# A hybrid mLSTM and attention block on one core: gates computed in the v/o projections, down weights requested earlier, stores of ScalarE's results issued on ScalarE's queue

## The chip, the cores and the metric

The kernel runs on one core of a Trainium2 chip. The metric is the device time of one execution in microseconds; the kernel before takes 3026.59 us, the median of three runs (3026.36 to 3028.20). Another execution, taken with the hardware profiler, gives the trace that all rows below come from.

## The reference

One layer of a bidirectional encoder for 2048 tokens of width 1024, all in float32:

```python
h = x
xn = rms_norm(h, ln_mix_g)
proj = xn @ w_in                                  # 2512 columns: q, k, v, o, gates, c_q, c_kv, k_rope
y_a = mlstm_group(q, k, v, o, gates + b_gates)    # 4 heads of 128, both directions, chunks of 128
y_b = mla_group(c_q, c_kv, k_rope, w_uq, w_ukv)   # 4 heads, softmax over all 2048 keys
h = h + concatenate([y_a, y_b]) @ w_out
h = h + (silu(conv3(xn2 @ w_up_gate)) * conv3(xn2 @ w_up_val)) @ w_down     # 2816 columns
h = h + sigmoid(rms_norm(h, ple_norm_g) @ w_ple_gate) * rms_norm(p @ w_ple_proj, ple_post_g)
return rms_norm(h, final_g)
```

The mLSTM's q and k go through a convolution over three tokens and a SiLU before use. Its gates (4 heads, two directions, an input and a forget gate) go through a logarithm of a sigmoid, running sums and running maxima along the tokens.

## The kernel before

Every large product is made of three matmuls (`mm3`, L127 to L132): both operands are split into a rounded high part and a rest, and high times high, high times low and low times high are added up in one PSUM bank. The split of an operand (`split`, L112, or `split_g`, which also scales) is a cast on ScalarE (L116 or L124) and a subtraction on VectorE (L119 or L125). Row L129 of a profile is therefore a matmul of any stage, and L116 and L119 are the splits of any operand; the tile names tell them apart: `wsp` and `xh`/`xl` are weights and x in the first projection, `woa`, `wq`, `cq` the operands of the side jobs, `q_t` the queries, `pt` transposed probabilities, `fw` the weights of the feed-forward part, `hid` its hidden values.

Intermediate results go to tensors in HBM (names that end in `_d`) and are read back when a later stage wants them. All transfers, loads and stores, are issued by SyncE (SP), which runs its instructions in program order: a transfer whose data or buffer is not ready holds up all that stand behind it. [...]

A scheduler sets the order of each engine's instructions from its own estimate of times, except for TensorE within `manual_schedule` (from L400 on, the q/k projection), where TensorE keeps the order of the code. Buffers are named places (`x0` to `x15`, `w0` to `w13`, `t0` to `t7`, `s0` to `s2`, `u0` to `u2`); a place is taken over by a new tile when the readers of the old one are done.

The stages, with their place in the profiled execution:

- `in_proj`, first part (0 to 120 us): x arrives transposed (`load_x`, L219), is squared (`x_sq`) for the row norms, split, and multiplied with the last 464 columns of w_in. `rest(st)` makes one row tile of 128 tokens; `turn_rest` (L275) transposes its results and stores them to `rest_d`.
- v and o projections (L315 to L331, 120 to 291 us): 16 row tiles each; `nat` makes the 24 matmuls of one tile.
- q/k projection (L333 to L436, 291 to some 520 us): for each of eight column groups j and four token ranges c, `block(j, c)` makes 24 matmuls, and `conv(j, c)` the three taps, the SiLU and the store to `qk_d` (L396). Between matmuls, `pump` (L368) draws steps from a chain of generators, `side`: `absorb` (L488: products of up-projection weights, stored to `wo_d`, L529), `gates` (L602: the scalar chain of the mLSTM gates, with matmuls on TensorE at L624, L640, L666, L676, L681, L701 and L707 that transpose or spread small tiles) and `q_up` (L533: queries for attention, stored to `q_d`). A `yield` ends a step; `pause(n)` is n empty steps. Each call of pump adds 1.26 steps, and there are four calls in a block. What is left of `side` after block(6, 2) is run off at once (L412).
- attention (`attend`, L926, some 520 to 1270 us): 64 query tiles (4 heads of 16) in turn. For each tile: four score banks on TensorE (`score_bank`), their maxima on VectorE (L884), exponentials on ScalarE (L902), transposes (L942), the split of `pt`, and after two tiles the products with the values (`pv`), whose result ScalarE copies to `ya` (L958) and SP stores with two DMAs to `y_d` (L960). Query tiles are loaded by `load_q` (L863) into `q_t`. Between them a slower pump draws steps from `tail` (L438) and `mlstm` (L711): a backward pass over 15 chunks, which stores transposed keys to `kn_d` (L761), and a forward pass over 16 chunks, which stores its result `hy` to `y_d` (L850).
- `out_proj` (1270 to 1450 us): the output projection, and the norm and transposition of its rows (`transpose_out`, L1038 to L1051), stored to `x2_d`.
- `up` (L1271, 1450 to 2290 us): 44 pairs of a gate and a value column group, each of seven products (`prod`) named after their operands. A pair's last products and its convolution (`rest`, `conv`) run within the next pair. `conv` works in two buffers `fgv` (w7 for the gate, w11 for the value), multiplies them into the value's one and stores it to `hid_d` (L1318). After the last pair, `down_weights` (L1409) starts the loads and splits of the first two down weights (`wd0`, L1393).
- `down` (2290 to 3027 us): 22 down weights times hidden values (`facc`) for each of four token ranges; in the last one the per-layer embedding is begun.

## Time and profile before

| what | us |
|---|---|
| median of three runs | 3026.59 |
| the profiled execution | 3029.05 |
| its span, first to last instruction | 3027.3 |
| TensorE busy (matmuls) | 2975.4 |
| VectorE busy | 1890.7 |
| ScalarE busy | 1360.7 |
| mean granted clock of TensorE, of full speed | 0.995 |

A wait in the profile is idle time of an engine just before an instruction, put down to what released that instruction. In a list of waits a row names the engine, the result and line of the instruction that waited, and the instruction it waited for, with the us in total, the number of times and the longest of them. In a table of windows a row gives a stretch in us from the span's start, its length, the busy time and number of instructions of five engines (TensorE's matmuls, its weight loads, VectorE, ScalarE, GpSimd), the clock granted to TensorE, the busy share of the DMA engines and the rate in GB/s.

### The profile page before, as it was taken

What the parts mean: (1) busy time and instruction counts of PE and PEld (TensorE: products, weight loads), DVE (VectorE), ACT (ScalarE), POOL (GpSimd) and SP (SyncE); (2) the same over time, 40 slices, a digit from 0 to 9 for tenths busy, and PEclk for the clock granted to TensorE, in tenths of its full rate; (3) what the DMA queues carried; (4) which work ended last, traced back from release to release, by engine and by line L of the source; (5) the groups of instructions that cost most, each with busy time, mean ns of one, the idle gap of its engine ahead of it and who ended that gap; (6) DMA issues with size and microseconds to landing.
All of it is one profiled execution on the core that took longest, in us unless ns stands there. A gap on an engine that the chain in (4) does not pass through costs nothing. (4 is left out here: it accounts for less than half of the span.)

```text
span 3027.3 us, 40574 instructions
## 1 busy us (share of the span) xinstructions
PE 2975.4 (98%) x15122; PEld 2510.5 (83%) x15122; DVE 1890.7 (62%) x3441; ACT 1360.7 (45%) x2602; POOL 142.0 (5%) x262
## 2 busy tenths in 40 slices
PE   8999999999999999999999999999999999999998
PEld 7888788898988888888778877888887888888887
DVE  7321655777776777646888888777776343334565
ACT  7211544555665566423534446444444332223443
POOL 3100000000000000001000000000000000000111
PEclk9999999999999999999999999999999999999999
DMA  6522345343323243568753335433337565444221
GB/s 194 110 70 96 109 135 162 121 150 107 105 93 93 96 126 114 178 207 274 229 194 134 135 135 194 140 122 123 124 122 233 164 221 199 146 155 148 79 79 63
DMA packets 322901, 430.03 MB, mean 142 GB/s; under 512 B 24960, under 2 KB 218512, under 8 KB 322704
## 3 DMA queue, kind: packets, MB, share of 16 engines
q1 hardware_dynamic: 322704, 427.44, 44.0%
q8 instruction: 119, 1.95, 0.3%
q14 instruction: 78, 0.64, 0.1%
HBM read 292.17 MB, written 135.20 MB: 141 GB/s over the span
## 5 line engine op out<-in xcount | busy, mean ns | idle before, releaser
L129 PE MATMUL facc<-fw,hid 128*128 128x512 f32 x2112 | 480.8, 389 | 3.7 <-ACT fw L116 2.6
L129 PEld LDWEIGHTS facc<-fw,hid 128*128 128x128 f32 x2112 | 396.0, 188 | 87.3 <-ACT fw L116 3.0
L129 PE MATMUL fxy<-oph,fw 128*128 128x512 f32 x1408 | 451.9, 394 | 6.0 <-DVE ug L1363 5.1
L129 PEld LDWEIGHTS fxy<-oph,fw 128*128 128x128 f32 x1408 | 265.7, 189 | 76.0 <-DVE ug L1363 11.7
L119 DVE TENSOR_TENSOR fw<-fwr,fw 128x1024 fp32r<-128x1024 f32 x176 | 215.1, 1222 | 166.8 <-ACT fw L116 166.6
L116 ACT CAST fw<-fwr 128x1024 fp32r<-128x1024 f32 x176 | 184.9, 1051 | 260.1 <-PE facc L129 131.4
L129 PE MATMUL fxy<-opl,fw 128*128 128x512 f32 x704 | 276.1, 392 | 0.0
L129 PE MATMUL bk<-wsp,xh 128*128 128x512 f32 (+1 forms) x768 | 235.9, 388 | 1.0 <-DVE wsp L125 1.0
L129 PE MATMUL fzs<-oph,fw 128*128 128x512 f32 x704 | 234.3, 389 | 0.9 <-DVE xt L1117 0.9
L116 ACT CAST pt<-tb 128x512 fp32r<-128x512 f32 x256 | 146.6, 586 | 195.2 <-PE tb L942 194.5
L884 DVE TENSOR_REDUCE mx<-bk 128x1 f32<-128x512 f32 x256 | 174.5, 684 | 48.3 <-PE bk L883 47.2
L129 PE MATMUL ppv<-pt,kv 128*128 128x256 f32 x1536 | 204.5, 287 | 0.0
L119 DVE TENSOR_TENSOR pt<-tb,pt 128x512 fp32r<-128x512 f32 x256 | 173.7, 684 | 36.9 <-ACT pt L116 35.0
L129 PEld LDWEIGHTS ppv<-pt,kv 128*128 128x128 f32 x1536 | 189.1, 191 | 0.3 <-ACT pt L116 0.3
L902 ACT ACTIVATE pe<-bk,nm 128x512 f32<-128x512 f32 x256 | 174.1, 695 | 24.5 <-DVE nm L896 23.7
L129 PE MATMUL pgp<-pw,x3s 128*128 128x512 f32 (+1 forms) x792 | 178.7, 385 | 0.0
L129 PE MATMUL bk<-wo,yhl 128*128 128x512 f32 x744 | 175.5, 392 | 0.0
L129 PEld LDWEIGHTS bk<-wsp,xh 128*128 128x128 f32 x768 | 145.4, 190 | 27.8 <-DVE wsp L125 2.7
L129 PEld LDWEIGHTS pgp<-pw,x3s 128*128 128x128 f32 x792 | 144.4, 188 | 28.3
L129 PEld LDWEIGHTS bk<-wo,yhl 128*128 128x128 f32 x744 | 138.2, 188 | 28.0
L129 PE MATMUL bk<-xh,wqk 128*128 128x512 f32 x480 | 159.0, 397 | 0.0
L129 PE MATMUL bk<-wsp,xl 128*128 128x512 f32 (+1 forms) x384 | 150.4, 392 | 8.0 <-ACT wsp L124 7.6
(324 smaller groups left out, 5363.5 us busy)
## 6 DMA issues: line engine op xcount, KB each, us to landing
fwr<-in_w_down SPq DMA_DIRECT2D x88, 512.0 KB, 3.6
fwr<-in_w_up SPq DMA_DIRECT2D x66, 512.0 KB, 4.1
s_d<-fwr SPq DMA_DIRECT2D x44, 512.0 KB, 3.3
fws<-s_d SPq DMA_DIRECT2D x44, 512.0 KB, 3.6
hraw<-hid_d SPq DMA_DIRECT2D x33, 512.0 KB, 4.3
rw<-row_d SPq DMA_DIRECT2D x32, 512.0 KB, 5.2
hid_d<-fgv SPq DMA_DIRECT2D x22, 512.0 KB, 3.5
hid_d<-fgv SPq DMA_DIRECT2D x22, 511.5 KB, 5.1
```

The source lines that it names most:

```text
L116: nc.scalar.copy(hi, src)
L119: (sub or nc.vector).tensor_tensor(lo, src, _f(hi), op=ALU.subtract)
L129: mm = lambda *a, **k: self.nc.tensor.matmul(*a, **k, skip_group_check=more)
L884: nc.vector.tensor_reduce(s.mx[:, kb:kb + 1], ps, axis=AX.X, op=ALU.max)
L902: nc.scalar.activation(s.pe[:, kb % 2], s.banks[kb], AF.Exp, bias=s.nm, scale=ASCALE, accum_out=s.rs[:, kb:kb + 1])
```

## The change

- `load_x(0)` is made with two DMAs of half the tile.
- `gates` is no longer part of `side`: a step of it is drawn after each row tile of the v projection from the third on and after each of the o projection; what is left is run off after these. Its own pauses are cut, its scratch tiles move from w5, w7, w8 and t6 to u0, u1, u2 and t4. `pump` adds 0.96 steps in place of 1.26; `absorb` begins with five empty steps in place of three, and its second result buffer moves from t7 to w2.
- `conv` is cut into `taps` (up to the SiLU) and `silu` (with the store). For the last column group, the three that were left at the end of the projection become steps of `tail`, hence side jobs of attention.
- 166 stores are issued by ScalarE (`nc.scalar.dma_start`): `rest_d`, `qk_d`, `wo_d`, `kn_d`, `y_d` of the mLSTM, `y_d` of attention, and `x2_d` in `out_proj`.
- In `up`, the two `fgv` buffers change places from pair to pair, and the product is written over the gate's.
- The first two down weights are requested within the last pair, the first after the product S1·T1 and the second after S2·T2, in places x13 and x14 (before x14 and x15), and no longer after the loop.

```diff
         def load_x(st):
-            nc.sync.dma_start(t, d["x_turned"][:, :, st * P:(st + 1) * P])
+            for f in range(1 if st else 2):
+                fs = slice(0, KT) if st else slice(4 * f, 4 * f + 4)
+                nc.sync.dma_start(t[:, fs], d["x_turned"][:, fs, st * P:(st + 1) * P])
...
-            nc.sync.dma_start(self.rest_d[:, :, st * P:(st + 1) * P], rt)
+            nc.scalar.dma_start(self.rest_d[:, :, st * P:(st + 1) * P], rt)
...
+        gates = self.gates()
...
             nc.sync.dma_start(self.v_d[st], t)
+            if st >= LAG_R:
+                next(gates, None)
...
             nc.sync.dma_start(self.o_d[st], t)
+            next(gates, None)
+        for _ in gates:
+            pass
...
-        side = chain(self.absorb(), self.gates(), self.q_up())
+        side = chain(self.absorb(), self.q_up())
...
-            due[0] += 1.26
+            due[0] += 0.96
...
+            silu(j, c, taps(j, c))
+
+        def taps(j, c):
             t = self.at(next(trot), [P, 512], name="ct")
...
+            return t
+
+        def silu(j, c, t):
             nc.scalar.activation(t, t, AF.Silu)
-            nc.sync.dma_start(self.qk_d[4 * c:4 * c + 4, :, j, :].rearrange("c p t -> p c t"),
+            nc.scalar.dma_start(self.qk_d[4 * c:4 * c + 4, :, j, :].rearrange("c p t -> p c t"),
...
             block(7, 1, self.gbank)
-            conv(7, 2)
             next(att)
             block(7, 0, self.gbank)
-            conv(7, 1)
-            conv(7, 0)
 
         def tail():
             for i in range(2):
                 self.split_kv(vals, (2 + i,))
                 yield
+            ts = []
+            for c in (2, 1, 0):
+                ts.append(taps(7, c))
+                yield
+            for c, t in zip((2, 1, 0), ts):
+                silu(7, c, t)
             yield from pause(6)
...
     def absorb(self):
-        yield from pause(3)
+        yield from pause(5)
...
-                o = self.at(f"t{6 + hf}", [P, 512], name="woo")
+                o = self.at(("t6", "w2")[hf], [P, 512], name="woo")
                 nc.scalar.copy(o, ps)
-                nc.sync.dma_start(self.wo_d[h, :, fs], o)
+                nc.scalar.dma_start(self.wo_d[h, :, fs], o)
...
     def gates(self):
-        mem = [self.at(f"w{i}", [P, 8, P], name="gtmp") for i in (5, 7, 8)]
-        mem.append(self.at("t6", [P, 4, P], name="gtm6"))
+        mem = [self.at(f"u{i}", [P, 8, P], name="gtmp") for i in range(3)]
+        mem.append(self.at("t4", [P, 4, P], name="gtm4"))
...
-        yield from pause(8)
+        yield
         pt = self.pml.tile([P, 2, 16], F32, name="gps", tag="ml")
         nc.tensor.matmul(pt, sel, mg, start=True, stop=True)
...
-            nc.sync.dma_start(self.kn_d[c], kk[:, 0])
+            nc.scalar.dma_start(self.kn_d[c], kk[:, 0])
...
-            nc.sync.dma_start(self.y_d[c, :, 0:4, :], hy[:, 1])
+            nc.scalar.dma_start(self.y_d[c, :, 0:4, :], hy[:, 1])
...
-                    nc.sync.dma_start(self.y_d[2 * pr + i, :, 4 + h, :], rb[:, i])
+                    nc.scalar.dma_start(self.y_d[2 * pr + i, :, 4 + h, :], rb[:, i])
...
     def transpose_out(self, xn, otag, dst, two=True):
-        nc.sync.dma_start(dst, xo)
+        nc.scalar.dma_start(dst, xo)
...
-                t = self.at(("w7", "w11")[half], [P, 2 * SB], name="fgv")
+                t = self.at(("w7", "w11")[half ^ s.i % 2], [P, 2 * SB], name="fgv")
...
-            tt(ts[1], ts[1], ts[0], op=ALU.mult)
+            tt(ts[0], ts[1], ts[0], op=ALU.mult)
...
             prod(s.z, s.ops["S1"], "T1")
+            if i == n - 1:
+                self.wdown = self.down_weights()
+                self.wd0 = [self.wdown(0)]
...
             prod(s.y, s.ops["S2"], "T2")
+            if i == n - 1:
+                self.wd0.append(self.wdown(1))
...
-        self.wdown = self.down_weights()
-        self.wd0 = [self.wdown(c) for c in range(2)]
         rest(prev)
         conv(prev)
...
     def down_weights(self):
-        self.wdrot, self.rrot = _rot("x", (14, 15, 13, 10, 11)), _rot("w", (0, 1))
+        self.wdrot, self.rrot = _rot("x", (13, 14, 15, 10, 11)), _rot("w", (0, 1))
```

The other pauses of `gates`, of two, three and six steps, become one step each or go; the rest of the diff puts the new product's name into the stores of `hid_d`.

More of the change, by code (lines that the diff above doesn't have):

```diff
@@ L621, in to_units @@
             V.tensor_copy(g.rearrange("p (r c h) -> p r h c", r=2, h=4), gt[:, :, f])
-            yield from pause(2)
+            yield
             pt = pbank()
@@ L663, in gates @@
         V.tensor_scalar(mg[:, 1], cm, g[:, P - 1:P], None, op0=ALU.mult)
-        yield from pause(8)
+        yield
         pt = self.pml.tile([P, 2, 16], F32, name="gps", tag="ml")
@@ L673, in gates @@
         flip(o, b)
-        yield from pause(3)
+        yield
         pt = self.pml.tile([P, 16], F32, name="gps", tag="ml")
@@ L694, in gates @@
             nc.sync.dma_start(self.row_d[:, i], o)
-        yield from pause(6)
+        yield
         for n, t in (("w", wl), ("e", em)):
@@ L698, in gates @@
             flip(o, t)
-            yield from pause(2)
+            yield
             pt = pbank()
@@ L704, in gates @@
         V.tensor_copy(sb, so.broadcast_to([P, P]))
-        yield from pause(2)
+        yield
         pt = pbank()
@@ L1315, in conv @@
                 ts.append(t)
-            tt(ts[1], ts[1], ts[0], op=ALU.mult)
+            tt(ts[0], ts[1], ts[0], op=ALU.mult)
             if b:
-                nc.sync.dma_start(self.hid_d[c, :, 2 * SB - 1:4 * SB - 1], ts[1])
+                nc.sync.dma_start(self.hid_d[c, :, 2 * SB - 1:4 * SB - 1], ts[0])
             else:
-                nc.sync.dma_start(self.hid_d[c, :, 0:2 * SB - 1], ts[1][:, 1:])
+                nc.sync.dma_start(self.hid_d[c, :, 0:2 * SB - 1], ts[0][:, 1:])
         def turn(s, f):
```

## The prediction

> **What bounds the kernel now.** I read the page's busy times first, then the waits of TensorE's matmuls by engine and line, then busy time by windows around the longest of these waits, and last the rows of single lines.

> ```profile
> span 3027.3 us, 40574 instructions
> PE 2975.4 (98%) x15122; PEld 2510.5 (83%) x15122; DVE 1890.7 (62%) x3441; ACT 1360.7 (45%) x2602; POOL 142.0 (5%) x262
> ```

> TensorE is busy for 98% of the span. The change removes no matmul, so all it can gain is in the 52 us in which TensorE has none (3027.3 − 2975.4), and in what a low clock adds to the busy time. The waits, as us in total, times, longest:

> ```profile
> PE bk L129 <- ACT wsp L124: 7.6, 1, 7.6
> PE fxy L129 <- DVE ug L1363: 5.1, 5, 3.1
> PE tb L942 <- DVE pt L119: 3.5, 11, 0.5
> PE bk L879 <- ACT pe L902: 3.4, 3, 2.5
> PE gps L666 <- DVE mg L662: 2.9, 1, 2.9
> PE facc L129 <- ACT fw L116: 2.6, 1, 2.6
> ...
> PE mb L738 <- issue: 2.1, 1, 2.1
> PE ssp L234 <- DVE x_ss L231: 1.9, 3, 1.5
> PE gb L512 <- DMA uqt<-in_w_uq_turned: 1.6, 1, 1.6
> PE gb L129 <- DVE woa L119: 1.4, 3, 0.8
> ...
> PE gps L701 <- DVE cols L702: 0.8, 1, 0.8
> ...
> PE gps L640 <- DVE u L372: 0.8, 1, 0.8
> ```

> These are few single events, not a steady loss. Five of them cost more than their length. The windows behind them (us; busy time and count of PE, PEld, DVE, ACT, POOL; the granted clock; DMA share and rate) show it, with two of the gaps themselves:

> ```profile
> 336.90:340.30 3.40, 3.40 (x9) 2.79 (x10) 0.50 (x3) 0.76 (x1) 0.00 (x0) 0.50 0.31 82
> 535.80:538.00 2.20, 0.08 (x2) 0.09 (x1) 2.09 (x7) 1.68 (x3) 0.00 (x0) 1.00 1.05 325
> 538.30:545.10 6.80, 6.21 (x18) 4.78 (x18) 2.64 (x7) 3.22 (x10) 0.00 (x0) 0.50 0.00 0
> 921.00:923.70 2.70, 0.19 (x2) 0.10 (x1) 0.80 (x3) 1.24 (x5) 0.00 (x0) 1.00 0.32 129
> 924.00:927.40 3.40, 3.40 (x10) 2.63 (x9) 0.76 (x2) 2.98 (x14) 0.25 (x2) 0.50 0.13 39
> 1575.90:1579.30 3.40, 3.40 (x9) 2.62 (x10) 3.40 (x5) 0.00 (x0) 0.00 (x0) 0.50 0.21 63
> 2292.70:2296.10 3.40, 3.40 (x9) 2.61 (x8) 3.40 (x4) 0.57 (x1) 0.00 (x0) 0.50 0.63 195
> ```

> After a gap of 2.5 to 3.1 us the clock is at 0.50 for 3.40 us (after the one at 535.8 for 6.80), in which TensorE does half its work: each such window costs another 1.7 us, the long one 3.4. So a gap that goes takes its window along. [...]

> **1. The gates move out of the q/k projection.** Before, this scalar chain ran between q/k matmuls, as a side job at 1.26 steps for each call of pump; after, it runs in the v/o projections, one step for each row tile, and pump goes at 0.96. The chain had waits of 2.9 (L666), 0.8 (L640) and 0.8 (L701), and behind the first lies the window at 336.9 (1.7): 6.2 us. Its new place, and the old one behind it:

> ```profile
> 206.00:291.00 85.00, 85.00 (x376) 70.09 (x375) 16.47 (x32) 16.18 (x32) 0.00 (x0) 1.00 0.25 87
> 323.00:358.00 35.00, 30.23 (x128) 23.90 (x127) 26.61 (x82) 17.46 (x29) 0.00 (x0) 0.95 0.30 86
> ```

> VectorE has work for 19% of the o projection, but for 76% of the stretch where the gates were. One row tile of the projection takes 85/16 = 5.3 us of matmuls, and VectorE's own part of it is 16.47/16 = 1.0. The longest link of the chain runs from the last gate's transposition to the matmul of L666, in the new order two row tiles, 10.6 us:

> ```profile
> L652 DVE SCALAR_TENSOR_TENSOR gtmp<-gtmp 128x128 f32<-128x128 f32 x8 | 2.3, 292 | 0.3
> ...
> L647 DVE RECIPROCAL gtmp<-gtmp 128x128 f32<-128x128 f32 x1 | 1.0, 952 | 0.0
> ```

> With these, some 14 more steps like those of L652 (14 × 0.29 = 4.1) and two tiles' own work (2.0) it comes to 9.4, and an exponential on ScalarE stands in it: there is hardly 1 us to spare, but a link that misses its tile delays TensorE only by the excess. I take no new wait (bounds 0 and the old 2.9 + 1.7). The absorbed weights start three pauses later, so the load of uqt is there when L512 wants it: 1.6. The woa waits (1.4) come from splits that are due every few steps; at 0.96 in place of 1.26 steps they have 31% more time: I take 1.2 of them. Against that, the side jobs now need 102 steps and get 104 × 0.96 = 99.8, so the last three are run off at once behind the last block that feeds them, and the transposes of qsr wait there for a VectorE chain with nothing between: bounds 0 and 2.9 (the longest that a VectorE chain held TensorE up here, L666), I take 1.2. **Sum of 1: −6.2 − 1.6 − 1.2 + 1.2 = −7.8**, between −9.0 and −1.5 (new waits of 2.9 + 1.7 in the o projection and 2.9 behind the drain, instead of 1.2).

> **2. Down weights asked for earlier.** In before, the first two down weights are split behind hid, and TensorE waits for the cast of the first:

> ```profile
> 2289.11 1.05 ACT L116 CAST hid<-hraw 128x1024 fp32r<-128x1024 f32 x1 [2.77 <-DMA hraw<-hid_d]
> ...
> 2291.29 1.99 ACT L116 CAST fw<-fwr 128x1024 fp32r<-128x1024 f32 x2
> ```

> ScalarE idles 2.77 us, casts hid, then does the first step of the last pair's convolution, and only then casts the two weights. Their loads depend on nothing made here. In the new order they are requested within the last pair, after two of its seven products, in buffers x13 and x14 that these products have released, and cast before hid, so TensorE needs no more than the one cast of hid at 2289.11 and can begin when that is done, some 2 us sooner, with more matmuls of this kind to do first: the 2.6 and its window (1.7) go. I take −3.8, leaving 0.5 for VectorE's part of hid; bounds −4.3 and 0 (if hid alone, whose load landed only for 2289.11, ends the same wait).

> **3. Stores on ScalarE's queue.** First the gain: SP issues all loads and stores in order, and a store at the head holds the loads behind it until ScalarE has made its data. The gap at 921 is such a case:

> ```profile
> 916.32 0.32 SPq L863 DMA_DIRECT2D q_t<-q_d  x1
> ...
> 922.46 0.40 ACT L116 CAST q_t<-q_t 128x256 fp32r<-128x256 f32 x1 [3.12 <-DMA q_t<-q_d]
> ```

> ScalarE sat 3.12 us before a cast whose load SP issued only at 916.32; the exponentials behind it, which give TensorE a score bank back, had to wait for it in ScalarE's order. What held SP:

> ```profile
> SPq L863 <- PE bk L883: 91.9, 25, 14.3
> ...
> SPq L960 <- ACT ya L958: 63.2, 16, 6.6
> ```

> The q_t load itself mostly waits for a matmul to release its buffer, so an SP without stores need not issue it sooner; but the y_d stores (L960) between such loads go. I take −3.8 of 2.5 + 1.7, bounds −4.2 and 0. Now the price. ScalarE issues these, each by what SP needs for it (ns min/median/max):

> ```profile
> L281 SPq DMA_DIRECT2D rest_d<-rt x16: 525/566/2062, 31.1 to 123.9; - x16
> L396 SPq DMA_DIRECT2D qk_d<-ct x32: 359/360/642, 307.5 to 534.1; - x32
> L529 SPq DMA_DIRECT2D wo_d<-woo x8: 319/324/447, 300.8 to 318.3; - x8
> L761 SPq DMA_DIRECT2D kn_d<-kk x15: 319/320/382, 534.8 to 674.9; - x15
> L850 SPq DMA_DIRECT2D y_d<-hy x16: 319/320/1413, 718.2 to 1267.4; - x16
> L960 SPq DMA_DIRECT2D y_d<-ya x64: 319/421/1382, 563.3 to 1256.4; - x64
> L1051 SPq DMA_DIRECT2D x_d<-nt_o x15: 525/525/1287, 1277.0 to 1447.6; - x15
> ```

> 16 × 0.566 + 32 × 0.360 + 8 × 0.324 + 31 × 0.320 + 64 × 0.421 + 15 × 0.525 = 68 us for 166 stores. [...] Where it lands:

> ```profile
> 560.00:920.00 360.00, 357.93 (x2451) 324.22 (x2450) 265.39 (x686) 212.81 (x576) 20.41 (x28) 1.00 0.38 116
> ```

> In attention ScalarE is busy for 59% and VectorE for 74% of 360 us, so 68 us over the 1300 us from 31 to 1447 have room on average. But the chain score bank, maximum, exponential, transpose, cast, matmul has no more slack than the 11 waits for pt (3.5 in all) show: it ends just in time. Lower bound 0, upper bound 68. It is nearest to the row of these 11 waits, since the same casts are pushed back, by about as much as one wait (0.3): I take a doubling, rounded down, **+3.0**.

> **4. The rest.** The first load of x in two halves: the wait of 7.6 ends with the cast of the first weight as much as with x, so I take −0.5 (bounds −2, the ssp wait of 1.9 gone, and +1.9, one more of them). The last convolutions go into the side jobs of attention: the L738 wait (2.1) ends with a pile of VectorE work (2.09 of the 2.20 us there), and the list of work that VectorE has before it is nearly the same in the new program: −0.5, bounds −5.5 (2.1 + 3.4) and +2.1. In up, the alternating fgv buffers leave TensorE's wait for ug (3.1 + 1.7) where it is, since the value half still writes what was just stored: 0, bounds −4.8 and 0.

> **The sum.** −7.8 − 3.8 − 3.8 + 3.0 − 0.5 − 0.5 = −13.4. The profiled execution took 3029.05 us (1.75 beside its span), 2.46 above the median of 3026.59, which I use: **3013 us** (3026.59 − 13.4).

> **Rivals.** (a) *The stores become the bound of attention*: every pair of ya stores stands in ScalarE's order ahead of exponentials and casts; if the 32 pairs reach TensorE whole, they cost 64 × 0.421 = 27 us, and 27 + 3026.6 − 13.4 − 3.0 = **3037**. It decides against the change when over 16.4/27 = 61% of this reaches TensorE. For it: one ScalarE instruction late by 3.12 stopped TensorE for 2.5 at 921. Against it: ScalarE's 41% idle time, and that the other exponentials wait for VectorE, not for ScalarE. (b) *The waits only move*: the gates' and the weights' own waits go, but 921 stays since its load waits for a matmul, the drain keeps TensorE for 2.9 in place of 1.2, and the stores cost twice what I take: −7.8 + 1.7 − 3.8 + 6.0 = −3.9, **3023**, which counts as the same. For it: the 91.9 us at L863. Against it: the stores that SP no longer has to wait for. (c) *More goes than I count*: 535 with its long window and the wait in up go too, and stores cost nothing: −13.4 − 3.0 − 5.0 − 4.8 = −26, **3000**. For it: both gaps end with VectorE work behind transfers that SP held. (d) *The queue change does nothing for the loads*: the transfers share the same engines, which show 38% of share in attention; then only the first two parts act and neither price nor gain of part 3 comes: 3026.6 − 7.8 − 3.8 − 1.0 = **3014**, the same time by another way. [...]

> **How the numbers follow.** Forecast, with (d) beside it, 0.52, own range 3006 to 3020; (a) 0.16; (b) 0.17; (c) 0.15. About 0.2%, 6 us, is what a measurement of this kernel can tell from no change, so faster is below 3020.5: 0.52 and 0.15 and a little of (b), 0.68; the same 0.17; slower 0.15. The range takes in (b), most of (c) and the lower half of (a): 3000 to 3033.

> **What would show it.** No wait at L666, L640 or L512 and a clock of 1.00 around 340 and 2290 show parts 1 and 2; a new wait of the qsr transposes shows the drain. In attention, q_t casts without a wait on their load show the gain of part 3, and the total of the waits of tb and bk there shows its price: 7 us or so if I am right, over 20 by (a). I am wrong if TensorE's busy time changes by more than the clock windows account for, or if the new order of the gates stops the o projection.

## The result, and the profile after

The changed kernel takes 3030.02 us (median of 20 runs, 3023.90 to 3035.60), the kernel before 3025.65 (20 runs, 3019.42 to 3029.69). The ratio is 1.0014 with a 95% interval of 1.0008 to 1.0020: slower by about 4 us, where 13 us less was forecast. The profiled execution of the changed kernel took 3035.60 us, the longest of its 20, so its single waits are read for their kind and place, and sums are left to the timed runs.

From the page of the changed kernel, the span and the busy times, and from its list of TensorE's waits (us in total, times, longest):

```profile
span 3033.8 us, 40494 instructions
...
PE 2973.5 (98%) x15122; PEld 2510.7 (83%) x15122; DVE 1891.8 (62%) x3441; ACT 1358.8 (45%) x2598; POOL 141.8 (5%) x262
```

```profile
PE bk L129 <- ACT wsp L124: 8.7, 1, 8.7
PE tb L1066 <- DVE xt L1053: 6.0, 5, 1.7
...
PE mb L755 <- DVE cb L759: 4.6, 2, 4.0
...
PE facc L129 <- DVE ug L1313: 3.1, 1, 3.1
PE bk L896 <- ACT pe L919: 2.9, 2, 2.2
PE mb L755 <- DVE kk L748: 2.8, 1, 2.8
PE gb L129 <- DVE uvs L119: 2.5, 1, 2.5
PE facc L129 <- DVE fw L119: 2.3, 1, 2.3
PE tb L612 <- DVE qsr L598: 1.5, 1, 1.5
...
PE facc L129 <- ACT fw L116: 1.2, 1, 1.2
```

TensorE is as busy as before, and its mean granted clock is 0.995 again; the waits have changed places. Those of the gates and of uqt are gone. New ones stand in the output projection (L1066), in the mLSTM's state products (L755), at the absorbed weights (uvs) and at the down weights (ug L1313 and the two fw rows). With the end of the last q/k matmul as the mark the changed kernel is 7.3 us ahead of the one before, and with the last product with attention's values 3.3. With the first product of `up` it is 3.5 behind, with the last of them 3.4 ahead again, and with the last `facc` 6.5 behind. So it loses time in attention, in the output projection and in `down`, and regains some in `up`.

### The profile page after: what moved, and what is told of

It is laid out like the page before. It is cut to its first block, busy times and chain, and to the rows that moved or that the text cites. A ratio compares the mean times of both kernels' runs of the same rounds, so it can differ in the third digit from the quotient of the medians.

```text
span 3033.8 us, 40494 instructions
## 1 busy us (share of the span) xinstructions
PE 2973.5 (98%) x15122; PEld 2510.7 (83%) x15122; DVE 1891.8 (62%) x3441; ACT 1358.8 (45%) x2598; POOL 141.8 (5%) x262
## 5 line engine op out<-in xcount | busy, mean ns | idle before, releaser
L129 PE MATMUL facc<-fw,hid 128*128 128x512 f32 x2112 | 484.7, 392 | 6.6 <-DVE ug L1313 3.1
L129 PEld LDWEIGHTS facc<-fw,hid 128*128 128x128 f32 x2112 | 399.4, 189 | 91.1 <-DVE ug L1313 3.5
L129 PE MATMUL fxy<-oph,fw 128*128 128x512 f32 x1408 | 450.1, 392 | 7.0 <-DVE ug L1385 5.4
L129 PEld LDWEIGHTS fxy<-oph,fw 128*128 128x128 f32 x1408 | 264.3, 188 | 76.3 <-DVE ug L1385 11.5
L119 DVE TENSOR_TENSOR fw<-fwr,fw 128x1024 fp32r<-128x1024 f32 x176 | 215.1, 1223 | 162.4 <-ACT fw L116 162.3
L116 ACT CAST fw<-fwr 128x1024 fp32r<-128x1024 f32 x176 | 184.9, 1051 | 261.2 <-PE facc L129 124.2
L129 PE MATMUL fxy<-opl,fw 128*128 128x512 f32 x704 | 275.0, 391 | 0.0
L129 PE MATMUL bk<-wsp,xh 128*128 128x512 f32 (+1 forms) x768 | 235.0, 387 | 1.1 <-DVE wsp L125 1.0
L129 PE MATMUL fzs<-oph,fw 128*128 128x512 f32 x704 | 234.4, 389 | 1.2 <-DVE xt L1134 1.2
L116 ACT CAST pt<-tb 128x512 fp32r<-128x512 f32 x256 | 146.9, 585 | 185.1 <-PE tb L959 184.6
L129 PE MATMUL ppv<-pt,kv 128*128 128x256 f32 x1536 | 203.9, 287 | 0.0
L119 DVE TENSOR_TENSOR pt<-tb,pt 128x512 fp32r<-128x512 f32 x256 | 174.1, 685 | 31.6 <-ACT pt L116 29.6
L129 PEld LDWEIGHTS ppv<-pt,kv 128*128 128x128 f32 x1536 | 189.0, 191 | 0.0
L129 PE MATMUL pgp<-pw,x3s 128*128 128x512 f32 (+1 forms) x792 | 178.7, 385 | 0.0
L129 PE MATMUL bk<-wo,yhl 128*128 128x512 f32 x744 | 175.5, 392 | 0.0
L129 PEld LDWEIGHTS pgp<-pw,x3s 128*128 128x128 f32 x792 | 144.4, 188 | 28.3
L129 PEld LDWEIGHTS bk<-wsp,xh 128*128 128x128 f32 x768 | 145.1, 190 | 27.3 <-DVE wsp L125 2.2
L129 PEld LDWEIGHTS bk<-wo,yhl 128*128 128x128 f32 x744 | 138.2, 188 | 28.1
L129 PE MATMUL bk<-wsp,xl 128*128 128x512 f32 (+1 forms) x384 | 151.0, 393 | 8.7 <-ACT wsp L124 8.7
L129 PE MATMUL bk<-xh,wqk 128*128 128x512 f32 x480 | 157.0, 393 | 0.0
```

The lines of the kernel that those rows point to most:

```text
L116: nc.scalar.copy(hi, src)
L119: (sub or nc.vector).tensor_tensor(lo, src, _f(hi), op=ALU.subtract)
L129: mm = lambda *a, **k: self.nc.tensor.matmul(*a, **k, skip_group_check=more)
```

## The experiments

The experiments are timed in five rounds, each beside the kernel before on the same chip; different groups of them ran on different chips, so rows are compared by their ratios. "us" is (ratio − 1) × 3025. An interval is 2 to 4 us to each side, so a difference of two rows is uncertain by 3 to 5 us, and the smaller ones below lean on the rows of the profiles beside them. A profile is of a single execution.

| kernel | median us | ratio, 95% interval | us |
|---|---|---|---|
| changed kernel | 3030.02 | 1.0014 [1.0008, 1.0020] | +4.2 |
| all stores on SP | 3021.77 | 0.9991 [0.9981, 1.0000] | −2.7 |
| corrected last rotation | 3024.53 | 1.0001 [0.9992, 1.0009] | +0.3 |
| x2 stores on SP | 3025.30 | 1.0004 [0.9996, 1.0013] | +1.2 |
| wo stores on SP | 3026.23 | 1.0005 [0.9994, 1.0015] | +1.5 |
| norm elsewhere | 3030.53 | 1.0018 [1.0008, 1.0028] | +5.4 |
| before, with the stores only | 3029.42 | 1.0016 [1.0008, 1.0025] | +4.8 |
| stores on SP, rotation corrected | 3019.57 | 0.9975 [0.9964, 0.9986] | −7.6 |
| the same, pause of three | 3015.43 | 0.9964 [0.9951, 0.9976] | −10.9 |
| stores on SP, late down weights | 3020.62 | 0.9984 [0.9975, 0.9993] | −4.8 |
| before, with the gates only | 3013.90 | 0.9960 [0.9948, 0.9973] | −12.1 |
| gates only, second time | 3015.63 | 0.9969 [0.9958, 0.9980] | −9.4 |
| gates, attention's stores | 3015.96 | 0.9967 [0.9953, 0.9981] | −10.0 |
| gates, convolutions in tail | 3020.20 | 0.9978 [0.9968, 0.9987] | −6.7 |
| gates, feed-forward edits | 3014.72 | 0.9965 [0.9952, 0.9978] | −10.6 |

**All stores back on SP.** The seven `nc.scalar.dma_start` become `nc.sync.dma_start` again.

> The changed kernel with all 166 stores back on SP; the rest of the change stays. If the queue change costs (the x2 stores delay the h1 stores of the output projection, 6.0 us of waits there; two wo_d stores stand ahead of a woa cast, 2.5 us and a clock window of 1.7), the time falls by 6 to 10 us against the changed kernel, to about 3022. If the stores on ScalarE's queue are free and the loss is all in the feed-forward part, it stays at 3030. If they bring the gain that was forecast at the query loads, it rises to about 3034.

6.9 us less than the changed kernel (4.2 + 2.7), within the 6 to 10 expected: the queue change costs.

**The stores alone, on the kernel before.** The other way round: seven `nc.sync` become `nc.scalar`.

> The kernel before with the 166 stores on ScalarE's queue and nothing else of the change. By the forecast (a gain of 3.8 at the query loads, a price of 3.0) 0 to -1 us against before. By the trace of the changed kernel it is slower by 5 to 10 us: about 6 in the output projection, the rest in the side jobs of the q/k projection and in attention. If ScalarE is the bound of attention, by 20 us or more.

Slower by 4.8 (2.4 to 7.6): just under the 5 to 10 that the trace gave, not the gain that was forecast, and far from a bound in attention. In its profile the output projection, from the last product with the values to the first of `up`, is 10 us longer than before (198.6 against 188.2).

**The x2 stores.** `nc.scalar.dma_start(dst, xo)` back to `nc.sync`, alone.

> The changed kernel with only the 15 x2_d stores of the output projection back on SP. If these transfers delay the h1 stores by running beside them, the five waits of the row transposes there (6.0 us) go and the time falls by 4 to 6 us, to about 3025. If ScalarE's own time for issuing them is what costs, the waits get shorter by 15 x 0.52 us of ScalarE at most and the DMA wait of VectorE stays near 30 us.

3.0 us less, where 4 to 6 were expected. VectorE's waits in the output projection, first before, then in the changed kernel, then in this one:

```profile
DVE xt L1036 <- DMA h_d<-xt: 13.8, 12, 1.8
```

```profile
DVE xt L1053 <- DMA h_d<-xt: 29.9, 12, 4.8
```

```profile
DVE xt L1053 <- DMA h_d<-xt: 16.1, 12, 1.9
```

The norm writes over rows that the h1 store still reads, so it waits for that transfer (29.9 us in total in the changed kernel). What changed beside it is in the lists of DMA issues (KB each, median us from issue to landing), before and in the changed kernel:

```profile
h_d<-xt SPq DMA_DIRECT2D x14, 512.0 KB, 2.9
x_d<-nt_o SPq DMA_DIRECT2D x14, 512.0 KB, 4.6
```

```profile
x_d<-nt_o ACTq DMA_DIRECT2D x13, 512.0 KB, 7.4
h_d<-xt SPq DMA_DIRECT2D x13, 512.0 KB, 3.6
```

Issued by SP, as the h1 stores are, the x2 stores landed 4.6 us after their issue; issued by ScalarE, 7.4. The median of the h1 stores says less: it is 3.6 too with the x2 stores back on SP, where the wait is 16.1. The increase lies in four of the rows, 9 to 12, in which `up` is prepared and reads x2 back: there VectorE waits 4.5, 4.8, 3.4 and 4.5 us, before 1.7 and less. From SyncE's, ScalarE's and VectorE's rows of the changed kernel's timeline, in row 10:

```profile
1386.62 0.32 SPq L1135 DMA_DIRECT2D h_d<-xt  x1
```

```profile
1386.78 0.52 ACTq L1068 DMA_DIRECT2D x_d<-nt_o  x1
```

```profile
1393.14 1.28 DVE L1053 SCALAR_TENSOR_TENSOR xt<-xt,rsr,g 128x1024 f32<-128x1024 f32 x1 [4.82 <-DMA h_d<-xt]
```

In rows 10 to 12 the x2 store is issued 0.2 to 1.7 us after the h1 store; in the earlier ones looked at it is 2.4 after it, and VectorE waits 1.5 as before. Whether the x2 store itself slows the h1 store there, or the reads of x2, which SyncE in row 10 now issues 1.7 us after it and before 4.4, is not separated.

**Norm elsewhere.** Is it this wait, or ScalarE's time for the issue?

```diff
-            self.norm_load(xt, g2, self.at(f"t{6 + c % 2}", [P, D], BF16, "junk"))
+            xn = self.at(f"w{2 + c % 2}", [P, D], name="xn") if 1 <= c <= 12 else xt
+            self.norm_load(xt, g2, self.at(f"t{6 + c % 2}", [P, D], BF16, "junk"), xn)
...
-            prev = (xt, "w11", self.x2_d[:, :, c * P:(c + 1) * P])
+            prev = (xn, "w11", self.x2_d[:, :, c * P:(c + 1) * P])
```

> The changed kernel, all stores on ScalarE's queue; the norm of the output projection (L1053) writes its result to another buffer for rows 1 to 12, instead of over the rows that the h1 store still reads. If the x2 stores cost because they hold up the h1 stores, the norm no longer waits for these, the waits of the row transposes (6.0) go and the time falls by 4 to 6 us to about 3025, although the x2 stores stay where they are. If ScalarE's time for issuing them costs, the waits stay and the time stays at 3030.

The waits went as expected and the time did not. From VectorE's, then TensorE's waits in the output projection:

```profile
DVE tsum L1193 <- DMA tsum<-x_d: 13.4, 4, 4.6
...
DVE xn L1053 <- POOL rsr L139: 10.4, 12, 1.2
DVE xt L1053 <- DMA h_d<-xt: 7.3, 2, 5.2
```

```profile
PE fzs L129 <- DVE xt L1134: 4.0, 1, 4.0
PE tb L1066 <- DVE xt L1053: 1.4, 1, 1.4
```

Where the norm has its own buffer it waits for no store, and of five waits of the transposes one is left, at row 0, which was not changed. But the wait comes back in a later row that was not changed either, and TensorE waits 4.0 at the first product of `up`. From VectorE's rows:

```profile
1436.69 1.28 DVE L1053 SCALAR_TENSOR_TENSOR xt<-xt,rsr,g 128x1024 f32<-128x1024 f32 x1 [4.29 <-DMA h_d<-xt]
...
1438.49 3.69 DVE L119 TENSOR_TENSOR opl<-opr,oph 128x512 fp32r<-128x512 f32 x6
...
1443.91 0.68 DVE L1134 TENSOR_TENSOR xt<-xt,bk 128x512 f32<-128x512 f32 x1
```

VectorE stands 4.29 us for the h1 store of row 14, then splits operands of `up`, and only then makes the sum (L1134) that TensorE waits for. So the store wait is shown to make the waits of the transposes; that its removal from rows 1 to 12 saves the 3 us is not.

**The wo stores.** Their line alone back on `nc.sync`.

> The changed kernel with only the 8 wo_d stores back on SP. If these two stores at a time, ahead of the cast of woa on ScalarE, make the wait of 2.5 us near 319 and the clock window behind it, both go and the time falls by 3 to 4 us, to about 3026. If the copies ahead of the stores are what comes late, or another store, the wait stays and so does the time.

The wait went, with 2.7 us, where 3 to 4 were expected. In the changed kernel's timeline (start, us, engine and line; in brackets the idle time before) it reads:

```profile
318.10 1.05 ACT L545 COPY woo<-gb 128x512 f32<-128x512 f32 x2
...
318.69 0.94 ACTq L546 DMA_DIRECT2D wo_d<-woo  x2
319.67 1.04 ACT L116 CAST woa<-wor 128x1024 fp32r<-128x1024 f32 x1 [0.53 <-ACT woo L545]
...
320.62 0.29 ACT L116 CAST uvs<-ukvt 128x128 fp32r<-128x128 f32 x1
```

ScalarE issues two stores for 0.94 us, then casts the next woa, then uvs, for which TensorE waits 2.5. The two places' 3.0 and 2.7 leave about 1 of the 6.9 to the others, less than the uncertainty.

**The last rotation.** Not foreseen by the forecast; in the changed kernel's timeline at the start of the last token range:

```profile
2666.65 1.04 ACT L116 CAST fw<-fwr 128x1024 fp32r<-128x1024 f32 x1
...
2667.75 0.96 PE L129 MATMUL facc<-fw,hid 128*128 128x512 f32 x3 [1.21 <-ACT fw L116]
...
2669.77 1.22 DVE L119 TENSOR_TENSOR fw<-fwr,fw 128x1024 fp32r<-128x1024 f32 x1
...
2671.04 2.50 PE L129 MATMUL facc<-fw,hid 128*128 128x512 f32 x5 [2.33 <-DVE fw L119]
```

The last range takes its weights' places from a rotation of its own, x13, x10, x11. With 66 weights before it and the old order 14, 15, 13, 10, 11, place 13 had been given out four weights earlier. In the new order 13, 14, 15, 10, 11 it belongs to the last weight of the range before, so the next split cannot begin until TensorE has used that one.

```diff
-                self.wdrot = _rot("x", (13, 10, 11))
+                self.wdrot = _rot("x", (10, 11, 13))
```

> The changed kernel, with the places of the down weights of the last token range taken in the order x10, x11, x13 instead of x13, x10, x11. If the two waits at 2667 (1.2 and 2.3 us) and the 6.8 us of half clock behind them come from the new start of the rotation, which hands x13 to the last weight of one range and the first of the next, they go and the time falls by 6 to 7 us, to about 3023. If they come from late loads, nothing changes.

3.9 us less, and neither wait in the profile; 6 to 7 were expected. In the profiles of the changed kernel and of the one with all stores on SP, `down` loses 5.8 and 5.0 us against the kernel before, counted from the 50th `facc` matmul to the last.

**Both corrections, and the mLSTM's start.**

> The changed kernel with all stores back on SP and the last rotation of the down weights in the order x10, x11, x13. If the two losses are separate places, both corrections add up: 8.3 (all stores back) and 5.5 (rotation) below the changed kernel's 3030.0, so about 3016, 9 us under the kernel before. If the corrections overlap, about 3021.

11.8 less than the changed kernel, though about 3016 was expected; the sum would be 10.8 (6.9 + 3.9), so the two are separate within the uncertainty. Against the gates alone (below) something is left. One place for it is attention. In the changed kernel's timeline:

```profile
657.81 0.44 SPq L788 DMA_DIRECT2D qk<-qk_d  x1
...
666.30 1.29 DVE L818 TENSOR_TENSOR qi<-qk,rw 128x512 f32<-128x512 f32 x2 [5.53 <-DMA qk<-qk_d]
667.51 0.68 DVE L901 TENSOR_REDUCE mx<-bk 128x1 f32<-128x512 f32 x1
668.11 0.60 DVE L759 SCALAR_TENSOR_TENSOR cb<-cb,cols,mb 128x129 f32<-128x129 f32 x2
```

VectorE stands 5.53 us at an instruction of the mLSTM whose load is on its way, and behind it in its order waits the sum that frees TensorE's bank: 4.05 us. The stores are not the reason, since it is there with all of them on SP (3.5). Three convolution steps now come ahead of the mLSTM, which so stands three steps later against the query tiles.

```diff
-            yield from pause(6)
+            yield from pause(3)
```

> Stores on SP, corrected rotation, and the six empty steps at the end of tail cut to three, so that the mLSTM's backward pass starts at the same step of attention as before the change, although three convolution steps come ahead of it. If the waits that are new in attention (663 and 848 us, with their clock windows) come from the mLSTM standing three steps later against the query tiles, 4 to 6 us go, to about 3011. If they come from the convolutions' work itself, nothing changes from 3016.

3.3 us less, which alone is within the uncertainty, and the waits of the state products for `cb` are gone from the list. But the wait at the query load, which the changed kernel does not have, is back (2.8). From the other side, the convolutions in tail, with six empty steps, on the kernel with the gates alone:

> The kernel with the gates moved only (3013.9), with the last three convolutions as steps of attention's side jobs and the six empty steps kept; stores on SP. If the mLSTM standing three steps later is what costs, the waits near 660 and 845 us come and the time rises by 4 to 6 us to about 3019. If those waits need the other parts of the change, it stays at 3014.

5.4 us more than the first run of the gates alone and 2.7 more than the second (below), 4.0 against their mean, with waits of 2.8 and 2.4 at 661 and 845 us. The sixteen profiles agree: the nine with the mLSTM three steps later have these two waits, one of 2.1 to 4.0 and one of 1.9 to 2.6, and none of TensorE's at the query load near 910; the seven others have that one, 2.0 to 2.8, and neither of the two.

**The gates alone, and the query load.** The hunks of the v/o projections, `pump`, `absorb` and `gates`, without the split load of x; stores on SP:

> The kernel before with the gates in the v/o projections, pump at 0.96 and what goes with it, nothing else of the change; stores on SP. By the forecast -7.8, to about 3018; by the changed kernel's trace about -9 up to the start of attention. If a later start of attention's side jobs gives it back there, about 3022 to 3025.

> The kernel with the gates moved only, a second time, beside the others on the same chip: 0.996 of the kernel before again, about 11 us less.

12.1 and 9.4 us less, more than the 7.8 that was forecast. With attention's 95 stores moved besides:

> The kernel with the gates moved only (3013.9), with the 95 stores of attention (kn_d, both kinds of y_d) on ScalarE's queue. By the forecast a gain of 3.8 at the query loads less a share of 3.0: about 3012, and the wait at 908 us (2.75) gone. If the query load there waits for its buffer and not for the stores ahead of it, the wait stays and the time is 3014 or, with the price of ScalarE's issues, up to 3017.

The same within the intervals, and the wait at the query load stays. From SyncE's and ScalarE's rows of this kernel's timeline:

```profile
906.13 0.32 SPq L869 DMA_DIRECT2D q_t<-q_d  x1
...
912.17 0.40 ACT L116 CAST q_t<-q_t 128x256 fp32r<-128x256 f32 x1 [3.04 <-DMA q_t<-q_d]
```

Without stores on SP the load lands 6.0 us after its issue, as before (916.32 to 922.46); TensorE waits 2.4. What held SyncE ahead of it is in its rows of the kernel before, the wait first:

```profile
SPq L774 <- PE mb L820: 14.1, 1, 14.1
```

```profile
899.23 0.80 SPq L960 DMA_DIRECT2D y_d<-ya  x2
900.12 0.38 SPq L771 DMA_DIRECT2D qk<-qk_d  x1
914.72 0.32 SPq L774 DMA_DIRECT2D cb<-cb_d  x1
915.78 0.32 SPq L780 DMA_DIRECT2D rw<-row_d  x1
916.32 0.32 SPq L863 DMA_DIRECT2D q_t<-q_d  x1
```

The stores (L960) were issued at 899.23. At the head of the queue stood a load of the mLSTM, `cb`, which waits 14.1 us until a matmul has read its buffer; with attention's stores moved it waits 16.3. This is why the place of the mLSTM decides on this wait and the stores do not.

**The down weights.**

> The changed kernel with all stores on SP and the down weights requested after the loop in the old places, as before. If the early request brings nothing of its own (the wait for the weight's cast is replaced by one for VectorE's last sum, L1313), this is as fast as the kernel with stores on SP and the corrected rotation, 3016. If the request is worth the forecast 3.8, this is 3.8 slower than that one, 3020.

> The kernel with the gates moved only, with the feed-forward edits added: alternating fgv buffers, the two down weights requested within the last pair, and the last rotation corrected to x10, x11, x13. If these edits are worth something once the rotation is right, the wait at 2275 (2.25) and its clock window go and it is 2 to 4 us faster than the gates alone; if the wait for the weight's cast only gives way to one for VectorE's last sums, it is the same within 1.5.

On one chip the feed-forward edits (10.6 less than before) cannot be told from the gates alone (9.4). Between the late request (4.8) and the early one (7.6) the intervals meet, so a gain of 2.8 is open. The changed kernel's timeline shows the wait that came instead:

```profile
2306.18 1.05 ACT L116 CAST hid<-hraw 128x1024 fp32r<-128x1024 f32 x1 [4.12 <-DMA hraw<-hid_d]
```

```profile
2307.27 1.23 DVE L119 TENSOR_TENSOR hid<-hraw,hid 128x1024 fp32r<-128x1024 f32 x1 [3.44 <-ACT hid L116]
2308.41 1.28 DVE L1327 SCALAR_TENSOR_TENSOR fgv<-uv,fcw,fgv 128x1024 f32<-128x1024 f32 x1
2309.61 0.68 DVE L1313 TENSOR_TENSOR ug<-ug,fzs 128x512 f32<-128x512 f32 x1
```

VectorE waits for a late hid ahead of the last pair's sum (L1313), and TensorE needs the banks which that sum frees: 3.1 us.

## Why the prediction was wrong

The sign was wrong. The gates gave more than was forecast, and the rest of the change lost more than that: the largest failed step is the price of part 3, looked for in attention and found elsewhere. That 3030 lies between the bounds of 3000 and 3033 says little, since these take in several rivals.

- **Part 1, the gates: right, and more than counted.** Forecast −7.8, measured −12.1 and −9.4. The waits at L666, L640, L701 and L512 are gone and the projections did not stop; the drain before the qsr transposes cost 1.5 where 1.2 was taken. With stores on SP no woa wait of 0.5 us or more is left. In the first profile of the gates alone the q/k projection is 11.5 us shorter than before: TensorE's idle time falls from 8.3 to 1.6 us and its busy time by 4.8, of which only the window's 1.7 was counted.
- **Part 2, the down weights: forecast −3.8.** The failing step was "TensorE needs no more than the one cast of hid": it needs the last pair's sums too, which stand on VectorE behind a later hid (3.1). What the early request is worth stays open: 2.8 by the pair of runs made for it, whose intervals meet. The forecast named the new places and did not follow them to the end of the rotation, a term that it put at nothing; it cost 3.9.
- **Part 3, the stores: forecast −0.8, measured +6.9 (undone) and +4.8 (alone).** Two steps failed. The gain rested on y_d stores that hold up the query load; what held it was a load of the mLSTM that waits for TensorE (14.1), and with attention's stores off SP the wait is still there. In the changed kernel's own trace this wait is gone, and casts of q_t without a wait were named as the sign of this gain. The sign misleads: with all stores back on SP TensorE does not wait there either, and with the mLSTM at its old place it does again. The price was looked for in attention, "nearest to the row of these 11 waits", where 95 stores cost nothing that can be told and the waits for pt went from 3.5 to 3.3. It lies where a store's neighbours were not looked at, the h1 store (3.0) and the cast of woa (2.7). The 68 us of issues were well estimated (71.1 in the changed kernel's trace), but in 37.1 of them ScalarE executes an instruction at the same time. Rival (a), a bound in attention, is out; rival (d), no effect, is out for the x2 and wo stores but right for attention's 95; rival (b), waits that only move, is the one it came near to, though by other waits than it named.
- **Part 4: forecast −0.5 for the convolutions, measured about +4 (2.7 to 5.4).** The step compared VectorE's work ahead of L738 and left out that the three steps move the whole mLSTM. For the split load of x −0.5 was forecast, and no run has it alone; in the profiles the first product of the projection starts at 8.3 to 9.3 us in the nine with it and at 7.3 to 7.6 in the seven without, so it loses 1 to 2 us there. The alternating fgv buffers were put at 0, and `up` lasts 863.4 us with them (gates, feed-forward edits) and 863.4 and 863.2 without (gates alone). That the wait of 3.1 in `up` is gone from the changed kernel is not their work: 2.9 is there in the same code with all stores on SP.

Put together by ratios: −10.7 (mean of the two gate runs) + 4.0 (convolutions, against that mean) + 6.9 + 3.9 = +4.1, against +4.2 measured. With 3 us of uncertainty and more in each term, so close a sum is luck; the early request of the down weights and the split load are not in it. One reading of the prediction is off without effect: from 31 to 1447 are 1416 us, not 1300.

## What to carry to other kernels

Before a store is moved to another queue, look at which transfers it will run beside, and at whose buffer waits for those: here, with the x2 stores on ScalarE's queue, the norm's waits for the h1 stores went from 13.8 to 29.9 us in total, and with them back on SP they are 16.1. Before a store is blamed for a late load, look at which instruction stood at the head of the queue, here a load that waited 14.1 us. In a pipeline of side jobs on counted steps, extra steps ahead of a job shift all of it against the main loop; take as many empty steps out, and follow a changed rotation to the place where another takes over from it. A list of edits that removes the visible waits should be tried edit by edit: here the gates alone are 15 us faster than all together.

## What was not expected of the hardware

```profile
920.60:924.00 3.40, 0.89 (x7) 0.65 (x6) 0.94 (x3) 1.54 (x5) 0.00 (x0) 1.00 0.36 145
```

```profile
905.90:909.30 3.40, 2.32 (x20) 2.13 (x18) 1.08 (x4) 0.58 (x2) 0.00 (x0) 1.00 0.82 269
909.30:912.70 3.40, 1.73 (x8) 1.43 (x9) 1.21 (x4) 2.87 (x9) 0.00 (x0) 1.00 0.17 57
912.70:916.10 3.40, 3.40 (x23) 2.98 (x22) 2.20 (x8) 2.30 (x12) 1.20 (x2) 1.00 0.23 82
```

TensorE is idle for 2.51 us of the first row, and for 1.08 and 1.67 us of the next two; in the last the clock is still 1.00. Over the 861 full clock steps of the kernel before, between 40 and 3005 us, the five in which TensorE was idle for 2.43 to 3.11 us were followed by half clock, and none of the others, with at most 1.27, was. Of the 861 of the changed kernel six were, with 1.89 to 2.45 us; one with 1.93 was not, and none of the others, with at most 1.40, was. The grid lies differently against these two executions: counted back towards the first instruction, its earliest border lies 2.38 us after it in the one and 1.05 in the other. That the same wait can have a window in one execution and none in another, and that part of a single profile's time is so chance, is the author's estimate from these rows. "A gap that goes takes its window along" thus holds only for the gaps that had one. Why some half clock stretches last one step (3.41 us) and others two (6.83 us, at 538.27 in the kernel before) stays open.
